# Dilated attention on one core: probabilities turned round by a matmul with a diagonal matrix of the reciprocal sums

## The chip, the cores and the metric

The kernel runs on one core of one Trainium2 chip. The time is device microseconds (us) of one execution, as the median of several runs. The engines named below are TensorE (PE; its weight loads are shown as PEld), VectorE (DVE), ScalarE (ACT), GpSimd (POOL) and SyncE (SP), which only issues transfers here.

## The reference, cut to what matters

The program is one inference step of a two-layer decoder: a layer of dilated attention and a layer of a state-space model, each followed by a SwiGLU. There are 512 prompt tokens, and 8 sample sequences of 8 tokens with caches of up to 2048 keys. The change lies in the attention. Its heart, in the reference:

```python
for g, (win, dil) in enumerate(((128, 1), (512, 4), (2048, 16))):
    s = einsum('bqhd,bqkhd->bqhk', q, k_gathered) * HEAD_DIM ** -0.5
    s = where(valid, s, -inf)
    lse = logsumexp(s, axis=-1)
    o = einsum('bqhk,bqkhd->bqhd', exp(s - lse), v_gathered)
    outs, lses = outs + [o], lses + [lse]
wts = softmax(stack(lses), axis=0)
o = einsum('gbqh,gbqhd->bqhd', wts, stack(outs))
```

Weighting the three groups by their softmax denominators is the same as one softmax over the keys of all three groups together. The kernel computes it so: one row maximum, one exponential and one sum for all keys of a query, and then one product with the values.

## The kernel before

All data are fp32. The program goes through stages in order: normalisation and the q, k, v projections, which also score the sample queries against the cached keys; attention; the output projection with the first feed-forward layer; the state-space layer; the second feed-forward layer. Projections split each fp32 operand into two parts and run three matmuls (`mm6`, L106). The attention stage lies at about 309 to 455 us of the profiled span.

**Prompt attention** (`prompt_pair`, L615) handles one pair of heads. For each of four residues r of the position modulo 4 (128 queries), PE writes a tile of scores S, 128 queries by 512 keys, for each head (L629, L632, L636). DVE adds the mask and takes the row maximum in one instruction (L641). Then `expnorm` (L606) negates and scales the maximum on DVE (L608), takes the exponential with a row sum on ACT (L610), the reciprocal on DVE (L612), and multiplies the 128 by 512 tile by it on DVE (L613). PE turns the four 128 by 128 blocks round (L645) with `te.transpose` against the identity, because the product with the values needs the keys on the partitions. ACT copies the first half of the result out (L646), DVE the second (L648). PE multiplies by the values (L652 for groups 1 and 2 inside the loop over r, L658 for group 0 behind it). There are 4 pairs, 4 residues and 2 heads, so 32 tiles and 128 transposes.

**Sample attention** (`decode`, L662) handles one of 8 sequences. Scores of all cached keys stand in `Sall`, 128 rows by 408. The same `expnorm` runs on them, PE turns three blocks of 128 keys and one of 24 (L671, L674), and PE multiplies with 13 blocks of cached values (L698) and one of new ones (L701). The values come from memory through a ring of six tiles (`kc`, up to 512 KB each), seven loads for a sequence (L388).

**Products.** For sequences 5 to 7 the scores of the widest group are still to be made here: `products` (L392) loads keys and a broadcast query, 512 KB each, into a second ring of four tiles. POOL multiplies them (L397) and DVE sums (L399). Four such parts make one sequence, which `close2` ends with a transpose on PE (L410).

The loop at L725 writes decode, prompt pair (with one product part ahead of each r), decode, four times. The order in which each engine's queue runs is not this order: the program is built with a scheduler that lays out all queues ahead of time by its own estimate of each instruction's duration. Each engine then runs its queue strictly in order, and SP issues transfers strictly in order.

Of the kernel before, what the change touches and what calls it, by code (L numbers as in the profile page):

```python
# [8 lines left out]
F32 = mybir.dt.float32  # L9
# [3 lines left out]
AF = mybir.ActivationFunctionType  # L13
OP = mybir.AluOpType
# [17 lines left out]
SCALE = HD ** -0.5  # L32
# [352 lines left out]
def cache_tile(nc, A, pool_, name, gi, b, c0, n, kv):  # L385
    t = pool_.tile([128, 2, 512], F32, name=name)[:, :n]
    st = STRIDE[gi]
    nc.sync.dma_start(t, dram(A[CACHES[gi]], (b * WIN[gi] + c0) * 1024 + kv * 512, [[st * 1024, 128], [1024, n], [1, 512]]))  # L388
    return t
# [200 lines left out]
def attn_phase(nc, tc, A, es, L):  # L590
    v, s, g, te = nc.vector, nc.scalar, nc.gpsimd, nc.tensor
    ident, pool = L["ident"], L["pool"]
    qT, kT, vt, vscr, att, Sall, mx3, mp, kst = (L[x] for x in ("qT", "kT", "vt", "vscr", "att", "Sall", "mx3", "mp", "kst"))
    ca = es.enter_context(pool("ca"))
    wk = es.enter_context(pool("wka", bufs=2))
# [7 lines left out]
    for t in Pz:  # L603
        g.memset(t, 0.0)

    def expnorm(sm, mx):  # L606
        nm = wk.tile([128, 1], F32, name="nm")
        v.tensor_scalar(nm, mx, -SCALE, None, op0=OP.mult)  # L608
        den = wk.tile([128, 1], F32, name="den")
        s.activation(sm, sm, AF.Exp, bias=nm, scale=SCALE, accum_out=den)  # L610
        rd = wk.tile([128, 1], F32, name="rd")
        v.reciprocal(rd, den)  # L612
        v.tensor_scalar(sm, sm, rd, None, op0=OP.mult)  # L613

    def prompt_pair(hp, fill):  # L615
        O = pO.tile([128, 4, 4, 32], F32, name="O")
        P0 = [wk.tile([128, 2, 4, 4, 32], F32, name=f"P0_{h}", bufs=1) for h in range(2)]
        for r in range(4):
            fill()
            P12 = {}  # L620
            S2 = [pS.tile([128, 512], F32, name="S") for _ in range(2)]
            half = [slice(0, 64), slice(64, 128)]
            for b in range(4):
                for h in range(2):
                    hs = half[h]
                    q = qT[0][hs, hp, r * 128 + b * 32:r * 128 + b * 32 + 32]
                    if b:
                        k = kT[0][hs, hp, (b - 1) * 128:(b + 1) * 128]
                        te.matmul(S2[h][b * 32:b * 32 + 32, 0:256], q, k, start=True, stop=True, tile_position=(h * 64, b * 32))  # L629
                    else:  # L630
                        k = kT[0][hs, hp, 0:128]
                        te.matmul(S2[h][0:32, 0:256].rearrange("p (a c) -> p a c", a=2), q, k[:, None, :].to_broadcast([64, 2, 128]), start=True, stop=True)  # L632
            for gi in (1, 2):
                sl = slice(r * 128, r * 128 + 128)
                for h in range(2):
                    te.matmul(S2[h][:, (gi + 1) * 128:(gi + 2) * 128], qT[gi][half[h], hp, sl], kT[gi][half[h], hp, sl], start=True, stop=True)  # L636
            for h in range(2):
                S = S2[h]
                sm = wk.tile([128, 512], F32, name="sm", bufs=3)
                mx = wk.tile([128, 1], F32, name="mx")  # L640
                v.tensor_tensor_reduce(sm, S, mp[:, r, :], 1.0, -3e38, OP.add, OP.max, mx)  # L641
                expnorm(sm, mx)
                pt = pP.tile([128, 4, 128], F32, name="pt")
                for c in range(4):
                    te.transpose(pt[:, c, :], sm[:, c * 128:(c + 1) * 128], ident)  # L645
                s.activation(P0[h][:, :, :, r, :], pt[:, 0:2, :].rearrange("p a (b i) -> p a b i", b=4), AF.Copy)  # L646
                p12 = wk.tile([128, 2, 128], F32, name="P12", bufs=3)
                v.tensor_copy(p12, pt[:, 2:4, :])  # L648
                P12[h] = p12
            for gi in (1, 2):  # L650
                for h in range(2):
                    te.matmul(O[h * 64:h * 64 + 64, r], vt[gi][:, r, (2 * hp + h) * 64:(2 * hp + h + 1) * 64], P12[h][:, gi - 1, :], start=gi == 1 and r == 0, stop=False, skip_group_check=True)  # L652
        for b in range(4):
            for pv in (1, 0):
                if b == 0 and pv == 0:
                    continue
                for h in range(2):
                    te.matmul(O[h * 64:h * 64 + 64, :, b, :], vt[0][:, b - 1 + pv, (2 * hp + h) * 64:(2 * hp + h + 1) * 64],  # L658
                              P0[h][:, pv, b], start=False, stop=True, skip_group_check=True)
        s.activation(att[:, hp, :T].rearrange("p (b i r) -> p r b i", b=4, r=4), O, AF.Copy)  # L660

    def decode(b):  # L662
        Z = Pz[b % 2]
        P = Sall[:, b].rearrange("p a b -> p (a b)")
        mx = wk.tile([128, 1], F32, name="mx")
        v.tensor_reduce(mx, mx3[:, b, :], AX.X, OP.max)
        expnorm(P, mx)
        P = Sall[:, b]
        pt = pD.tile([128, 4, 128], F32, name="Sd")
        for c in range(3):  # L670
            te.transpose(pt[:, c, :], P[:, c, 0:128], ident)  # L671
        pw = dk.tile([128, 24], F32, name="pw")
        v.tensor_copy(pw.rearrange("p (a b) -> p a b", a=3), P[:, :, 128:136])
        te.transpose(pt[:24, 3, :], pw, ident)  # L674
        pa = dk.tile([128, 4, 32], F32, name="pa")
        s.activation(pa, pt[:, 0, :].rearrange("p (a c) -> p a c", a=4), AF.Copy)
        pn = dk.tile([24, 128], F32, name="pn")
        s.activation(pn, pt[:24, 3, :], AF.Copy)
        for gi, u0, n in ((1, 0, 4), (2, 4, 8)):
            for h in range(2):  # L680
                for m in range(8 // n):
                    j0 = h * 8 + m * n
                    base = Z[:, u0, :, j0:j0 + 1]
                    o = bass.AP(tensor=base.tensor, offset=base.offset, ap=[list(base.ap[0]), [32, 4], [129, n]])
                    v.tensor_copy(o, pt[:, gi, :].rearrange("p (a c) -> p a c", a=4)[:, :, j0:j0 + n])
        vn = dk.tile([24, 512], F32, name="vn", bufs=2)
        for gi in range(3):
            nc.sync.dma_start(vn[gi * 8:gi * 8 + 8, :], vscr[gi, b * 8:b * 8 + 8, :])
        O = pD.tile([128, 128], F32, name="Sd")
        u = 0  # L690
        for gi in (0, 1, 2):
            for c0 in range(0, UNITS[gi], 2):
                w = min(2, UNITS[gi] - c0)
                vc = cache_tile(nc, A, kst, "kc", gi, b, c0, w, 1)
                for c in range(w):
                    for hp in range(4):
                        pz = pa[:, hp, :] if u == 0 else Z[:, u - 1, hp, :]
                        te.matmul(O[hp * 32:hp * 32 + 32, :], pz, vc[:, c, hp * 128:hp * 128 + 128], start=u == 0, stop=False, tile_position=(0, hp * 32), skip_group_check=True)  # L698
                    u += 1
        for hp in range(4):  # L700
            te.matmul(O[hp * 32:hp * 32 + 32, :], pn[:, hp * 32:hp * 32 + 32], vn[:, hp * 128:hp * 128 + 128], start=False, stop=True, tile_position=(0, hp * 32), skip_group_check=True)  # L701
        os_ = dk.tile([128, 128], F32, name="os")
        s.activation(os_, O, AF.Copy)
        ot = pD.tile([128, 4, 32], F32, name="Sd")
        te.transpose(ot.rearrange("p a b -> p (a b)"), os_, ident)
        q0 = T + b * 8
        for h in range(2):
            hs = slice(h * 64, h * 64 + 64)
            v.tensor_copy(att[hs, :, q0:q0 + 8], ot[hs, :, h * 8:h * 8 + 8])
# [15 lines left out]
    for hp in range(4):  # L725
        decode(2 * hp)
        prompt_pair(hp, score2)
        decode(2 * hp + 1)
# [623 lines left out]
```

## Time and profile before

| what | value |
|---|---|
| median of 3 runs | 1567.87 us (1565.44 to 1578.34) |
| the profiled execution, its own time | 1561.29 us |
| its span from first to last instruction | 1559.5 us |
| attention stage within the span | about 309 to 455 us |
| mean granted TensorE clock | 0.990 |

In the views, a group row has the line, engine, operation, output and inputs, sizes, count, and after the bar the busy time in us, the mean of one in ns, and the idle time ahead of it with what ended it. A row of waits says which engine and line waited for what: us in total, times, longest. Matmul ends are modelled and a matmul's duration includes the time it takes through the array, so consecutive ones overlap; what the next one has to wait is seen in the distance from start to start.

### The profile page before, as it was taken

The numbers are of one execution on the slowest core, as the hardware profiler recorded it, in microseconds if no ns is written. First come the engines' busy times: TensorE is split into PE (matmuls) and PEld (weight loads), VectorE is DVE, ScalarE is ACT, GpSimd is POOL, SyncE is SP. The second block draws the span as 40 slices with busy tenths as digits, with TensorE's granted clock in tenths as the row PEclk, the third lists the DMA queues.
The fourth block names the chain that finished last, engine by engine and source line by source line (L and its number), as shares of the span: only waits on it lengthen the run. The fifth ranks groups of instructions, "written<-read, shape, count | busy, mean of one in ns | idle before, by whom it ended". The sixth has DMA issues, their size and how long they took to land. (4 is left out here: it accounts for less than half of the span.)

```text
span 1559.5 us, 28913 instructions
## 1 busy us (share of the span) xinstructions
PE 1504.5 (96%) x12010; PEld 1393.8 (89%) x12010; DVE 917.9 (59%) x1661; ACT 522.4 (33%) x774; POOL 318.3 (20%) x343
## 2 busy tenths in 40 slices
PE   8989899889979999999999999999999999999998
PEld 6878688656669999999999999999999999999998
DVE  5898864558726865388878667764443333333332
ACT  4524344634415221122222254443342212221222
POOL 2000102333203014745335420021111001000100
PEclk9999999999989999999999999999999999999999
DMA  7497753798785556589667765964655555442212
GB/s 248 143 375 234 264 187 109 239 357 285 275 274 195 189 189 223 202 283 315 213 241 243 237 227 181 287 204 170 215 189 189 188 188 220 153 145 82 82 62 81
DMA packets 194323, 326.79 MB, mean 210 GB/s; under 512 B 39568, under 2 KB 137104, under 8 KB 192656
## 3 DMA queue, kind: packets, MB, share of 16 engines
q1 hardware_dynamic: 184112, 305.86, 57.8%
q10 hardware_dynamic: 10080, 19.08, 3.5%
q8 instruction: 94, 1.54, 0.4%
q14 instruction: 37, 0.30, 0.1%
HBM read 291.31 MB, written 120.88 MB: 264 GB/s over the span
## 5 line engine op out<-in xcount | busy, mean ns | idle before, releaser
L100 DVE TENSOR_TENSOR wlo<-raw,whi 128x1024 fp32r<-128x1024 f32 x200 | 246.4, 1233 | 269.1 <-ACT whi L99 263.3
L106 PE MATMUL acc<-xgl,whi 128*128 128x288 f32 x1760 | 378.6, 296 | 1.0 <-DVE xgl L171 1.0
L106 PE MATMUL acc<-xgh,wlo 128*128 128x288 f32 x1760 | 377.7, 296 | 0.0
L106 PE MATMUL acc<-xgh,whi 128*128 128x288 f32 x1760 | 377.0, 296 | 0.1
L99 ACT ACTIVATE whi<-raw 128x1024 fp32r<-128x1024 f32 x200 | 208.1, 1042 | 503.3 <-PE acc L106 405.0
L106 PEld LDWEIGHTS acc<-xgl,whi 128*128 128x128 f32 x1760 | 282.6, 188 | 2.5 <-DVE xgl L171 1.3
L106 PEld LDWEIGHTS acc<-xgh,wlo 128*128 128x128 f32 x1760 | 282.7, 188 | 0.6 <-issue 0.2
L106 PEld LDWEIGHTS acc<-xgh,whi 128*128 128x128 f32 x1760 | 281.7, 188 | 0.5 <-DVE gt L789 0.3
L791 POOL TENSOR_TENSOR gt<-gt,rstd 128x576 f32<-128x576 f32 x44 | 77.1, 1754 | 431.8 <-ACT gt L790 431.7
L106 PE MATMUL acc<-hh,whi 128*128 128x288 f32 x704 | 151.3, 296 | 0.0
L106 PE MATMUL acc<-hh,wlo 128*128 128x288 f32 x704 | 151.2, 295 | 0.0
L106 PE MATMUL acc<-hl,whi 128*128 128x288 f32 x704 | 150.9, 295 | 0.0
L352 PE MATMUL acc<-wlo,xh 128*128 128x512 f32 x288 | 115.6, 403 | 3.2 <-DVE wlo L100 3.2
L351 PE MATMUL acc<-whi,xh 128*128 128x512 f32 x288 | 108.8, 402 | 5.0 <-ACT a L567 3.9
L106 PEld LDWEIGHTS acc<-hh,wlo 128*128 128x128 f32 x704 | 113.2, 188 | 0.2 <-issue 0.2
L106 PEld LDWEIGHTS acc<-hl,whi 128*128 128x128 f32 x704 | 113.0, 188 | 0.2 <-issue 0.2
L353 PE MATMUL acc<-whi,xl 128*128 128x512 f32 x288 | 113.1, 398 | 0.0
L106 PEld LDWEIGHTS acc<-hh,whi 128*128 128x128 f32 x704 | 113.1, 188 | 0.0
L191 POOL TENSOR_TENSOR ssum<-ssum,sq 128x576 f32<-128x576 f32 x21 | 36.1, 1720 | 181.0 <-ACT sq L190 181.0
L351 PEld LDWEIGHTS acc<-whi,xh 128*128 128x128 f32 x288 | 54.9, 192 | 18.3 <-ACT a L567 4.7
L352 PEld LDWEIGHTS acc<-wlo,xh 128*128 128x128 f32 x288 | 55.3, 192 | 15.4 <-DVE wlo L100 4.2
L803 DVE TENSOR_TENSOR xT<-acc,xT 128x576 f32<-128x576 f32 x48 | 36.2, 754 | 49.2 <-PE acc L106 49.2
(349 smaller groups left out, 2010.8 us busy)
## 6 DMA issues: line engine op xcount, KB each, us to landing
o_kv_s<-cache_kv_w SPq DMA_DIRECT2D x64, 1020.0 KB
kc<-cache_kv_w SPq DMA_DIRECT2D x96, 512.0 KB
raw<-ffn_w_gate SPq DMA_DIRECT2D x44, 512.0 KB
raw<-ffn_w_up SPq DMA_DIRECT2D x44, 512.0 KB
raw<-ffn_w_down SPq DMA_DIRECT2D x40, 512.0 KB
raw<-w_qkv SPq DMA_DIRECT2D x36, 512.0 KB
kc<-qscr SPq DMA_DIRECT2D x32, 512.0 KB
o_kv_s<-cache_kv_w SPq DMA_DIRECT2D x16, 1008.0 KB
```

The source lines that it names most:

```text
L99: s.activation(hi, raw, AF.Copy)
L100: mark[0] = v.tensor_tensor(lo, raw, hi.bitcast(F32), OP.subtract)
L106: te.matmul(ps[:, c, :HN], w, x[:, c * HN:(c + 1) * HN], start=first and i == 0, stop=last and i == 2)
L191: g.tensor_tensor(self.ss, self.ss, sq, OP.add)
L351: te.matmul(ps[t], ah, wh[:, k2, :], start=k == 0, stop=False)
L352: te.matmul(ps[t], ah, wl[:, k2, :], start=False, stop=False)
L353: te.matmul(ps[t], al, wh[:, k2, :], start=False, stop=k == KT - 1)
L791: g.tensor_tensor(t, t, nin.r, OP.mult)
L803: v.tensor_tensor(xv, ps[m][:, :, :HN], xv, OP.add)
```

## The change

In `expnorm` the scaling of the whole tile by the reciprocal sum is gone. In its place DVE scales the 128 by 128 identity by the reciprocal sums, which gives a diagonal matrix `dg`, and PE's four `te.transpose` calls become ordinary `te.matmul` calls with `dg` as the moving operand. Turning round and normalising are one step. In the prompt part, the masking instruction now also multiplies by minus the scale and takes the minimum, so that it gives the negated maximum directly; the exponential then uses a scale of -1. In the sample part the negation stays as its own instruction. No transfer is added or removed.

```diff
-    def expnorm(sm, mx):
-        nm = wk.tile([128, 1], F32, name="nm")
-        v.tensor_scalar(nm, mx, -SCALE, None, op0=OP.mult)
+    def expnorm(sm, nm, scale):
         den = wk.tile([128, 1], F32, name="den")
-        s.activation(sm, sm, AF.Exp, bias=nm, scale=SCALE, accum_out=den)
+        s.activation(sm, sm, AF.Exp, bias=nm, scale=scale, accum_out=den)
         rd = wk.tile([128, 1], F32, name="rd")
         v.reciprocal(rd, den)
-        v.tensor_scalar(sm, sm, rd, None, op0=OP.mult)
+        dg = wk.tile([128, 128], F32, name="dg", bufs=3)
+        v.tensor_scalar(dg, ident, rd, None, op0=OP.mult)
+        return dg
...
-                mx = wk.tile([128, 1], F32, name="mx")
-                v.tensor_tensor_reduce(sm, S, mp[:, r, :], 1.0, -3e38, OP.add, OP.max, mx)
-                expnorm(sm, mx)
+                nm = wk.tile([128, 1], F32, name="nm")
+                v.tensor_tensor_reduce(sm, S, mp[:, r, :], -SCALE, 3e38, OP.add, OP.min, nm)
+                dg = expnorm(sm, nm, -1.0)
                 pt = pP.tile([128, 4, 128], F32, name="pt")
                 for c in range(4):
-                    te.transpose(pt[:, c, :], sm[:, c * 128:(c + 1) * 128], ident)
+                    te.matmul(pt[:, c, :], sm[:, c * 128:(c + 1) * 128], dg, start=True, stop=True)
...
-        expnorm(P, mx)
+        nm = wk.tile([128, 1], F32, name="nm")
+        v.tensor_scalar(nm, mx, -SCALE, None, op0=OP.mult)
+        dg = expnorm(P, nm, SCALE)
...
-            te.transpose(pt[:, c, :], P[:, c, 0:128], ident)
+            te.matmul(pt[:, c, :], P[:, c, 0:128], dg, start=True, stop=True)
...
-        te.transpose(pt[:24, 3, :], pw, ident)
+        te.matmul(pt[:24, 3, :], pw, dg, start=True, stop=True)
```

The scheduler lays the queues of the attention stage out anew; ahead of the last cache scores and from the first matmuls of the output projection on, PE's queue is unchanged. Two places in the queues matter below. (In the new kernel the exponential of `expnorm` is L608, the reciprocal L610 and the diagonal L612, and from L667 on a line of the kernel before stands two lines further down.)

The first is DVE's queue in the first head pair. The kernel before has one product part (the two sums of L399) between the work on the second and third residue:

```order
391 L608 TENSOR_SCALAR nm<-mx 128x1
392 L641 ISA sm,mx<-S,mp 128x512
393 L641 ISA mx 128x1
394 L709 COPY att<-Sd 64x4x8 x2
395 L608 TENSOR_SCALAR nm<-mx 128x1
396 L612 RECIPROCAL rd<-den 128x1
397 L399 TENSOR_REDUCE P_3317<-kc 128x4x2 x2
398 L613 TENSOR_SCALAR sm<-sm,rd 128x512
```

The new kernel has all four parts of sequence 5 there, ahead of the masking of the second residue's second head and of the first two copies of L648:

```order
383 L641 ISA sm,nm<-S,mp 128x512
384 L641 ISA nm 128x1
385 L610 RECIPROCAL rd<-den 128x1
386 L399 TENSOR_REDUCE P_3318<-kc 128x4x2 x2
387 L612 TENSOR_SCALAR dg<-ident,rd 128x128
388 L399 TENSOR_REDUCE P_3318<-kc 128x4x2 x6
389 L641 ISA sm,nm<-S,mp 128x512
390 L641 ISA nm 128x1
391 L648 COPY P_3356<-pt 128x256
392 L648 COPY P_3373<-pt 128x256
```

What moved: three more product parts stand ahead of the rest of the second residue.

The second is the end of PE's queue in the attention stage. The kernel before has two whole sample sequences behind the last prompt products (L658):

```order
1395 L658 MATMUL O<-P_1_4783,vt_3165 64x4x32
1396 L698 MATMUL Sd<-kc,pa 32x128 x4
1397 L698 MATMUL Sd<-kc,Pz_3203 32x128 x48
1398 L701 MATMUL Sd<-vn,pn 32x128 x4
1399 L705 MATMUL Sd<-ident,os 128x128
1400 L671 MATMUL Sd<-ident,Sall 128x128 x3
1401 L674 MATMUL Sd<-ident,pw 24x128
1402 L698 MATMUL Sd<-kc,pa 32x128 x4
1403 L698 MATMUL Sd<-kc,Pz_3204 32x128 x48
1404 L701 MATMUL Sd<-vn,pn 32x128 x4
1405 L705 MATMUL Sd<-ident,os 128x128
1406 L106 MATMUL acc_5178<-ath,whi 128x288 x2
```

The new kernel has one:

```order
1399 L658 MATMUL O<-P_1_4766,vt_3165 64x4x32
1400 L700 MATMUL Sd<-kc,pa 32x128 x4
1401 L700 MATMUL Sd<-kc,Pz_3204 32x128 x48
1402 L703 MATMUL Sd<-vn,pn 32x128 x4
1403 L707 MATMUL Sd<-ident,os 128x128
1404 L106 MATMUL acc_5154<-ath,whi 128x288 x2
```

What moved: the seventh sequence's products with the values stand further up, between prompt work.

## The prediction

> **What bounds the kernel now.** I read the page first, to see which engine is full, then the attention stage in windows, then who waits there. On the page PE is busy 96% of the span, DVE 59%. The change touches only the attention stage, so the stage decides. Its windows (busy us and count of each engine, granted clock, DMA share, GB/s):
>
> ```profile
> core 0: us, PE busy (x) PEld busy (x) DVE busy (x) ACT busy (x) POOL busy (x), PEclk, DMA share, GB/s
> 309.00:327.00 18.00, 11.10 (x198) 8.33 (x198) 3.62 (x25) 5.47 (x11) 3.44 (x17) 0.81 1.03 377
> 327.00:437.00 110.00, 104.41 (x1445) 68.73 (x1449) 84.55 (x305) 48.68 (x132) 30.00 (x20) 0.98 0.83 293
> 437.00:455.00 18.00, 10.93 (x206) 6.78 (x206) 1.15 (x9) 0.98 (x4) 0.00 (x0) 0.81 0.85 283
> ```
>
> There are three parts. Up to 327 us PE has gaps and the transfers run at 377 GB/s; from 327 to 437 PE is busy 104 of 110 us; behind that it has gaps again. DVE is at 85 of 110 us in the middle, high but second. Since a matmul's shown duration holds its way through the array, I checked the middle in the timeline (start, duration):
>
> ```profile
> 356.10 0.66 PE L645 MATMUL pt<-ident,sm 128*128 128x128 f32 x4
> 356.69 0.40 PE L632 MATMUL S<-kT,att 64*32 64x256 f32 x1
> ...
> 357.25 0.71 PE L636 MATMUL S<-kT,qT 64*128 64x128 f32 x4
> 357.89 0.33 PE L410 MATMUL Sd<-ident,P 128*128 128x128 f32 x1
> ```
>
> Each piece starts before the one ahead of it is out of the array. What PE waits for, in the middle window (first eight rows) and in the last one (two rows):
>
> ```profile
> PE S L632 <- DVE mx L641: 1.3, 2, 1.0
> PE pt L645 <- ACT pa L676: 1.2, 1, 1.2
> PE O L652 <- DVE P L648: 0.8, 1, 0.8
> PE O L652 <- DVE nm L608: 0.6, 1, 0.6
> PE pt L645 <- DVE sm L613: 0.6, 1, 0.6
> PE pt L645 <- ACT P L646: 0.6, 1, 0.6
> PE Sd L698 <- DMA kc<-cache_kv_w: 0.2, 1, 0.2
> PE pt L645 <- DVE pw L673: 0.2, 1, 0.2
> ...
> PE Sd L698 <- DMA kc<-cache_kv_w: 5.7, 6, 2.4
> PE Sd L705 <- ACT os L703: 0.9, 2, 0.5
> ```
>
> In 110 us PE waits 3.5 us for DVE, 1.8 for ACT and 0.2 for a transfer: 5.5 us. Nearly all of the rest is PE's own work. So I read the middle as bound by PE, and the end, 5.7 us, by the loads of cached values.
>
> **The change on PE.** The question is what an ordinary fp32 matmul costs beside a transpose. Rows of the whole span and of the stage:
>
> ```profile
> L645 PE MATMUL pt<-ident,sm 128*128 128x128 f32 x128 | 20.3, 289 | 2.6 <-ACT pa L676 1.2 <-DVE sm L613 0.6 <-ACT P L646 0.6
> L652 PE MATMUL O<-P,vt 128*64 128x128 f32 x128 | 16.7, 291 | 1.5 <-DVE P L648 0.8 <-DVE nm L608 0.6
> ...
> 666.27 0.60 PE L1039 MATMUL aux<-ident,wr 128*128 128x128 f32 x4
> ...
> L1039 PE MATMUL aux<-ident,wr x64: 270/272/329, 666.3 to 866.6; 128*128 128x128 f32 x64
> ...
> 988.95 0.34 PE L1174 MATMUL aux<-U,Tc 128*128 128x72 f32 x2
> ...
> 995.83 0.39 PE L1175 MATMUL acc<-Xt,Vc 128*128 128x72 f32 x2
> ```
>
> L645 stands in the code 4 x 4 x 2 x 4 = 128 times and has 128 records: a transpose is one instruction. L652 stands there 4 x 4 x 2 x 2 = 64 times and has 128 records: an ordinary fp32 matmul is two. The price of a transpose comes from L1039: four take 0.60 us, the last of them 0.272, so the step is (0.60 - 0.272) / 3 = 0.109 us. The price of an ordinary one with a full 128 by 128 stationary operand comes from the stretch of L1174 and L1175: from the first to the last row there are 32 calls, of L1174 and L1175 in turn, so 31 steps: (995.83 - 988.95) / 31 = 0.222 us. These have 72 moving columns instead of 128; two instructions of a transpose's step, which has 128, would be 0.218, so I see no reason for a very different price. So a new call takes 0.113 us more. [...] There are 128 calls in the prompt part and 8 x 4 = 32 in the sample part, so PE gets 160 x 0.113 = +18.1 us. The bounds are 0, if the second instruction runs in gaps that PE has anyway, and 18.1, if none does. Eight calls, those of the first and last sequence, stand beside waits for transfers: -0.9.
>
> **The change on DVE and ACT.**
>
> ```profile
> L613 DVE TENSOR_SCALAR sm<-sm,rd 128x512 f32<-128x512 f32 x32 | 22.4, 701 | 0.5
> L399 DVE TENSOR_REDUCE P<-kc 128x8 f32<-128x512 f32 x24 | 15.2, 677 | 2.0 <-POOL kc L397 2.0
> L608 DVE TENSOR_SCALAR nm<-mx 128x1 f32<-128x1 f32 x40 | 5.5, 143 | 0.1
> L613 DVE TENSOR_SCALAR Sall<-Sall,rd 128x408 f32<-128x408 f32 x8 | 4.4, 556 | 0.1
> ```
>
> Removed: 22.4 + 4.4 us of L613, and 32 of the 40 negations, 32 x 0.143 = 4.6 us; together 31.4. Added: 40 diagonals of 128 by 128. No row shows one. The nearest rows are L608 at 0.143 and L613 at 0.556; the two forms of L613 differ by 0.145 us for 104 elements, so 128 elements come to 0.556 - 280 x 0.0014 = 0.17. I take 0.2 (bounds 0.14 and 0.56): 8 us. DVE is relieved of about 23 us. The exponential with another scale and the minimum in place of the maximum keep their sizes, so I cost them at nothing; ACT, at 49 of 110 us, would hide a small change.
>
> But DVE's relief is worth only what PE waits for it. The chain from scores to transposes gets shorter by 0.143 + 0.5 us for each tile, and of the 5.5 us in the middle I let 3.0 go (bounds 0 and 5.3). What is late next is PE itself.
>
> **The order.** At the end, one sample sequence instead of two stands behind the prompt work, so the loads of the seventh can run under it. Of the 5.7 us of load waits and 0.9 of the last copies I let 4.0 go (bounds 0 and 6.6). At the front, the new kernel starts prompt scores ahead of the first sequence's values, and puts four product parts into DVE's queue ahead of the second residue. Queued behind them on DVE are a masking and the two copies (L648) for which PE's value products wait. What the parts take:
>
> ```profile
> L397 POOL TENSOR_TENSOR kc<-kc 128x1024 f32<-128x1024 f32 x12 | 28.4, 2371 | 48.4 <-DMA kc<-qscr 36.8 <-ACT P L646 11.5
> L698 PE MATMUL Sd<-kc,Pz 128*32 128x128 f32 x768 | 29.8, 294 | 6.0 <-DMA kc<-cache_kv_w 5.9
> ```
>
> Four parts load eight tiles of 512 KB, 4.2 MB; at 293 GB/s that is 14.3 us, and a multiplication (2.4) and two sums (1.4) follow the last: 18 us. PE has the first sequence's values to run there, 29.8 / 8 = 3.7 us, and eight blocks of turning, 8 x 0.222 = 1.8. If nothing else covers it, the hold is 18 - 5.5 = 12.5 us. On the other side, an earlier start of the scores can give back at most what PE waits at the front for loads of keys:
>
> ```profile
> PE pt L484 <- DMA kc<-cache_kv_w: 6.2, 2, 3.4
> ```
>
> The bounds are -6.2 and +12.5. The product parts that come early are not in the way later, and the loads are the same in sum, so I take 0.
>
> The sum: 18.1 - 0.9 - 3.0 - 4.0 + 0 = +10.2 us. On the profiled execution, whose own time is 1561.29 us for a span of 1559.5, that is 1571.5. The median of the three runs is 1567.87, 6.6 us above it; I add to the median: 1578.
>
> **The rivals.**
>
> *DVE sets the pace, and the kernel gets faster.* For it speaks that DVE is at 85 of 110 us and that ACT waits for DVE's negation often:
>
> ```profile
> ACT sm L610 <- DVE nm L608: 31.0, 22, 5.5
> ```
>
> If the second instruction of a new call slips into gaps on PE (those between its pieces, which the wait rows leave out), the 18.1 us vanish and what PE waits for is won: up to 5.5 in the middle and 6.6 at the end, 12.1 us, 1556. It decides where a call costs less than 12.1 / 160 = 0.076 us more than a transpose. Against it stand the rows at 0.113 and PE's short waits. Chance 0.10, taken over -5 to -12.
>
> *Hidden.* PE's addition falls into waits for loads, since the first 20 us of the stage move 377 GB/s and the middle 293; the transfers, not PE, then set the end. Against it: one wait of 0.2 us for a transfer in the middle. -5 to +4, about 1567. Chance 0.13.
>
> *Fourfold.* [...] Chance 0.02.
>
> *The front holds.* The product parts keep DVE and then PE for the 12.5 us worked out: 10.2 + 12.5 = +22.7, 1590. For it speaks the strict order of the queues; against it, that PE gets ahead elsewhere. Taken over +15 to +23. Chance 0.17.
>
> The forecast, PE pays for most of the second instructions, +4 to +15, has 0.58.
>
> **How the numbers follow.** A change of under 1% (15.7 us) can't be told from none with three runs that lie 13 us apart. Faster by more than that needs more than all of PE's waits: 0.03, out of the first rival. Slower by more than that is nearly all of the last rival, the fourfold one and a little of the forecast's upper edge: 0.21. Within 1%: 0.76. The range reaches from the lower side of "hidden" (-5, 1563) to the upper of "the front holds" (+23, 1591); outside lie most of the first rival and the fourfold one, 0.12, and a little for the unknown terms.
>
> **What would show it.** The rows of the turning should have 256, 48 and 16 records in place of 128, 24 and 8, with about 0.22 us from call to call. DVE's busy time in the stage should fall by about 23 us and the waits of PE for it by some 3. The load waits ahead of the output projection should shrink to 1 or 2 us. The first matmul of the output projection should come about 10 us later; all behind it should be unmoved. A wait of many us of PE for L648 or L641 in the first head pair would be the front's hold. A start-to-start step near 0.11 us per call would prove the price wrong.

## The result, and the profile after

The changed kernel takes 1593.12 us (median of four, 1592.34 to 1599.11) where the kernel before, run beside it, takes 1572.14 us: 21.0 us more, a ratio of 1.0155 with a 95% interval of 1.0117 to 1.0193. In a later session, with more executions (e13 below), the medians are 1595.34 and 1573.55 us and the ratio 1.0131 (1.0093 to 1.0169). The ratios leave out a run that lies more than 1.5% above the fastest one of its kernel. The forecast was +10.2 us; the loss is about twice that, and close to the +22.7 of the rival "the front holds".

The profiled execution after took 1599.11 us for a span of 1597.0, 37.8 us more than the profiled one before. That is more than the medians differ by, and the sections below show most of why: the two executions spent different times at half clock.

First the page's windows of the kernel after. The columns are those of the windows in the prediction: busy us and count of each engine, granted clock, DMA share, GB/s. The stage was cut where its character changes:

```profile
321.00:345.00 24.00, 18.08 (x173) 11.42 (x174) 6.71 (x29) 4.44 (x11) 6.14 (x12) 0.52 0.83 282
345.00:353.00 8.00, 1.92 (x52) 1.57 (x48) 1.81 (x3) 0.00 (x0) 2.23 (x2) 0.71 0.86 284
353.00:366.00 13.00, 13.00 (x80) 8.55 (x74) 6.92 (x18) 2.67 (x7) 6.13 (x7) 0.50 1.04 386
366.00:386.00 20.00, 20.00 (x222) 14.33 (x222) 17.33 (x53) 8.68 (x24) 7.09 (x3) 0.99 0.59 202
386.00:490.00 104.00, 99.45 (x1420) 72.14 (x1417) 47.98 (x192) 36.73 (x99) 10.21 (x8) 1.00 0.66 230
```

And the same stage of the kernel before:

```profile
317.00:325.00 8.00, 6.11 (x88) 4.86 (x91) 0.62 (x4) 1.79 (x3) 0.61 (x3) 0.57 1.05 386
325.00:333.00 8.00, 7.89 (x154) 4.21 (x147) 3.96 (x15) 2.28 (x7) 0.00 (x0) 1.00 1.05 393
333.00:356.00 23.00, 21.11 (x212) 13.57 (x210) 21.62 (x71) 11.29 (x31) 9.38 (x4) 1.00 0.67 245
356.00:456.00 100.00, 88.23 (x1336) 58.81 (x1334) 60.66 (x232) 36.67 (x102) 20.61 (x16) 0.95 0.85 294
```

The first head pair ends at 356 us before and at 386 after, 30 us later. Of these, 6 us lie ahead of its first scores, which start at 325.7 us before and at 332.0 after; in e13, the changed kernel once more, they start at 326.9, so these 6 us belong to this execution and not to the change. From its first score to its last product the pair takes 31 us before, 54 after and 51 in e13. The rest of the stage, which holds three quarters of the new second instructions, takes 100 us before and 106 after (the output projection starts at 456 and at 492 us). So most of the loss is at the front. The granted clock there is 0.50 to 0.52 for most of 45 us, where the front before has a low clock only in the 8 us from 317.

What PE waits for from 309 to 385 us in the kernel after:

```profile
PE Sd L700 <- DMA kc<-cache_kv_w: 6.1, 1, 6.1
PE pt L484 <- DMA kc<-cache_kv_w: 5.0, 1, 5.0
PE Sd L673 <- DVE dg L612: 1.3, 1, 1.3
PE Sd L488 <- DVE mx L493: 1.1, 2, 0.5
PE S L632 <- DVE mx L493: 0.4, 1, 0.4
```

Both long waits are for transfers: one for a late tile of cached keys, and one for the seventh value tile of the first sequence. Only the second is new: for key tiles the kernel before waits 6.2 us, in two waits (the prediction shows the row). No wait for L648 or L641 of the first head pair is among them. The value ring holds six tiles. In the new order PE makes the scores of two residues before it touches the first value tile, so the seventh can only be asked for late. In e13 PE waits 9.3 us for that tile, with a clock of 0.88 from 350 us to the pair's end at 378, and the pair takes 51 us all the same: half clock alone is not the front's loss.

Finally the turning itself (the tile's view, then three rows of PE's timeline: start, duration), and the diagonals:

```profile
L645 PE MATMUL pt<-dg,sm x256: 274/275/583, 341.8 to 481.0; 128*128 128x128 f32 x128
...
354.40 3.35 PE L645 MATMUL pt<-dg,sm 128*128 128x128 f32 x14
...
369.32 1.16 PE L645 MATMUL pt<-dg,sm 128*128 128x128 f32 x8
370.40 0.62 PE L629 MATMUL S<-kT,att 64*32 64x256 f32 x2
```

```profile
L612 DVE TENSOR_SCALAR dg<-ident,rd 128x128 f32<-128x128 f32 x40 | 19.4, 485 | 13.0 <-PE pt L645 12.0
```

There are 256 records for 128 calls: two instructions each, as forecast. At full clock four calls take 370.40 - 369.32 = 1.08 us up to the next piece. In the kernel before, four transposes took 356.69 - 356.10 = 0.59. So a call costs 0.49 / 4 = 0.122 us more, and 160 calls 19.6 us; the prediction had 0.113 and 18.1. At half clock seven calls (354.40 to 357.68) take 0.47 us each.

### The profile page after: what moved, and what is told of

Read it like the earlier page. It is cut to its first block, busy times and chain, and to the rows that moved or that the text cites. A ratio compares the mean times of both kernels' runs of the same rounds, so it can differ in the third digit from the quotient of the medians.

```text
span 1597.0 us, 29201 instructions
## 1 busy us (share of the span) xinstructions
PE 1540.0 (96%) x12170; PEld 1424.1 (89%) x12170; DVE 910.7 (57%) x1629; ACT 522.6 (33%) x774; POOL 316.8 (20%) x343
## 5 line engine op out<-in xcount | busy, mean ns | idle before, releaser
L353 PEld LDWEIGHTS acc<-whi,xl 128*128 128x128 f32 x288 | 55.5, 193 | 11.2
```

Of the source, the lines that this page charges most:

```text
L353: te.matmul(ps[t], al, wh[:, k2, :], start=False, stop=k == KT - 1)
```

## The experiments

Two theories were set against each other at first. "Price": the loss is the second instruction of 160 matmuls. "Front": the loss is the order at the front of the stage, and that order comes from where the tiles lie in memory. The second has a reason in the build. The three `dg` tiles take 1536 bytes per partition, and everything allocated behind them moves up by that much. The accumulator of the product parts, P2, lay on an operand of the projections before; now it lies in part on tiles that the scoring of cached keys still uses, as Q2 does. A buffer that comes free later gives the scheduler another order; which of the overlaps decides was not tried. As built, with one `dg` buffer (512 bytes) the order of the front is like that of the kernel before, with two (1024 bytes) like that of the kernel after; neither was timed.

**e1, the tiles shifted and nothing else.** The kernel before, with unused room at the end of two tiles:

```diff
-        P0 = [wk.tile([128, 2, 4, 4, 32], F32, name=f"P0_{h}", bufs=1) for h in range(2)]
+        P0 = [wk.tile([128, 1216], F32, name=f"P0_{h}", bufs=1)[:, :1024].rearrange("p (a b r i) -> p a b r i", a=2, b=4, r=4) for h in range(2)]
```

> The kernel before with no operation changed: the two tiles P0 of the prompt attention are each 768 bytes per partition longer than they need be, 1536 bytes together, as much as the three diagonal tiles of the changed kernel take. That shifts the sample part's small tiles and the ring of the product parts to the addresses that they have in the changed kernel, and the order that the scheduler then writes has four product parts ahead of the second residue's second masking, as there. Theory 'front' (the changed kernel's loss comes from the order at the front of the attention stage, and the order comes from where the tiles lie): +12 to +30 us, about as much as the whole change (+21), and the end of the first head pair about 25 to 30 us later than before. Theory 'price' (the loss is the second instruction of 160 matmuls): within 3 us of the kernel before.

Measured: 1589.22 against 1566.54 us, ratio 1.0121 (1.0078 to 1.0165), about +19 us by the ratio and +23 by the medians. On another chip (e15) it was 1.0109 (1.0066 to 1.0151). No operation differs from the kernel before, so the new order is worth nearly the whole change by itself, and "price" as the only cause falls. Windows of e1, and PE's longest waits from 320 to 393 us:

```profile
320.00:343.00 23.00, 18.51 (x201) 12.24 (x205) 7.66 (x32) 4.44 (x11) 6.67 (x12) 0.55 0.85 286
343.00:351.00 8.00, 1.79 (x44) 0.99 (x32) 1.65 (x4) 0.00 (x0) 2.35 (x1) 0.67 0.91 303
351.00:393.00 42.00, 42.00 (x216) 23.95 (x210) 25.84 (x85) 12.34 (x33) 17.22 (x11) 0.50 0.72 246
393.00:483.00 90.00, 84.41 (x1335) 58.04 (x1331) 50.41 (x211) 36.28 (x98) 5.57 (x6) 0.99 0.74 249
```

```profile
PE Sd L698 <- DMA kc<-cache_kv_w: 6.2, 1, 6.2
PE pt L484 <- DMA kc<-cache_kv_w: 3.6, 1, 3.6
```

PE waits 6.2 us for the seventh value tile. Then it is busy 42.00 of 42 us, with no listed wait of its own, at a granted clock of 0.50. The first head pair takes those 42 us; in the kernel before its turnings and products took the 23 us from 333. The shift brings the new order of the end too, with one sample sequence behind the prompt work, and there time comes back: the rest of the stage takes 90 us, with 100 in the kernel before (at a clock of 0.99 and 0.95). So the front by itself costs more than the +19.

**e2, the changed kernel with its diagonals allocated last.**

```diff
+    dgp = es.enter_context(pool("dgp", bufs=3))
...
-        dg = wk.tile([128, 128], F32, name="dg", bufs=3)
+        dg = dgp.tile([128, 128], F32, name="dg")
```

> The changed kernel with its three diagonal tiles in a pool of their own, allocated behind the product parts' ring: every other tile lies where it lay before, and the order of the front is nearly that of the kernel before. All operations are those of the changed kernel. Theory 'front': the loss of the front goes; what is left is the second instructions less what DVE's relief gives, -5 to +11 us against the kernel before. Theory 'price': +18 to +21 us, as the changed kernel.

Measured: 1577.50 us, ratio 1.0076 (1.0047 to 1.0106), about +12 us. All other tiles lie where they lay, the front is back, and what is left is close to the +10.2 that the prediction gave with the order term at zero. That is partly luck: by the table below some 4 us of less time at half clock are in it, and the rest is +15. Its windows and PE's waits from 327 to 471 us:

```profile
321.00:333.00 12.00, 9.80 (x202) 6.29 (x197) 3.64 (x18) 3.31 (x7) 1.27 (x7) 1.00 1.02 357
333.00:361.00 28.00, 28.00 (x292) 19.55 (x286) 22.08 (x65) 12.16 (x33) 9.40 (x4) 1.00 0.76 268
361.00:471.00 110.00, 103.27 (x1463) 73.37 (x1460) 55.46 (x209) 37.79 (x101) 20.50 (x16) 0.98 0.79 263
...
PE Sd L701 <- DMA kc<-cache_kv_w: 4.2, 5, 1.5
...
PE pt L646 <- DVE dg L613: 0.3, 1, 0.3
```

From 321 us on the front runs at full clock, and PE waits 0.3 us for a diagonal.

**e3, the second instruction alone.** `te.transpose(…, ident)` became `te.matmul(…, ident, start=True, stop=True)` at the three places, and DVE's scaling and negations stayed.

> The kernel before with one edit: the 160 turnings of the probabilities are ordinary fp32 matmuls with the identity in place of transposes; the scaling on DVE and the negations stay. The front's order is close to the kernel before. If PE pays for each second instruction (0.113 us by the prediction): +15 to +18 us. If the second instructions run in gaps that PE has anyway: -2 to +5 us. Theory 'front' leaves room for anything up to +10.

Measured: 1576.57 us, ratio 1.0050 (1.0019 to 1.0081): +8 us by the ratio, +10 by the medians. That is less than the 15 to 18 expected. The table below has one reason; another is that the end has the new order here too (from the last prompt product to the output projection PE takes 8.4 us in e3, 20.7 in the kernel before), so this run does not hold the second instruction quite alone.

**e4, the negated maximum alone.** The masking instruction of the kernel before got `-SCALE`, `3e38` and `OP.min`, and 32 negations went.

> The kernel before with the other part alone: the masking instruction of the prompt part gives the negated maximum itself, and 32 negations go (32 x 0.143 = 4.6 us of DVE). Turnings and scaling as before. Both theories: the chain from scores to turning is shorter by 0.14 us in each of 32 tiles, and PE waits 3.5 us for DVE in the whole middle, so -3 to 0 us; a change beyond 3 us either way would be the order again, which differs from the second residue on.

Measured: 1570.67 us, ratio 1.0013 (0.9983 to 1.0044): nothing that can be told from zero. The relief of DVE that this part brings has no price here.

**e5, the product parts taken apart.** The changed kernel, with each part's sums behind the previous residue's copy:

```diff
-            fill()
+            if hp == 0 and r:
+                with tc.issue_after(last.ins):
+                    fill()
+            else:
+                fill()
...
-                v.tensor_copy(p12, pt[:, 2:4, :])
+                last = v.tensor_copy(p12, pt[:, 2:4, :])
```

> The changed kernel with one rule more on the order: in the first head pair the sums of a product part come on DVE behind the copy (L648) of the residue before, so that each residue has one part ahead of its masking and not four. All operations stay. Theory 'hold' (what the prediction's rival said: four parts keep DVE, and PE waits for its maskings and copies): 10 to 15 us of the changed kernel's loss go, which leaves +8 to +12 us against the kernel before. Theory 'clock' (PE first waits for two transfers, a key tile and the seventh value tile, and then runs at half clock with no long wait): those two waits stay, so the loss stays, +17 to +25 us.

Measured: 1590.22 us, ratio 1.0129 (1.0070 to 1.0187), the same as the changed kernel (1.0131). DVE's waits for POOL's product, kernel after from 335 to 386 us (first row) and e5 from 309 to 386 (second), and PE's two waits in e5 (last two):

```profile
DVE P L399 <- POOL kc L397: 16.0, 4, 6.8
```

```profile
DVE P L399 <- POOL kc L397: 3.3, 1, 3.3
...
PE pt L484 <- DMA kc<-cache_kv_w: 6.1, 1, 6.1
PE Sd L704 <- DMA kc<-cache_kv_w: 5.6, 1, 5.6
```

The hold on DVE went, from 16.0 us to 3.3, and no time came back that the runs can show; the interval reaches down to +11 us, so a few us could hide in it. In the changed kernel itself no long wait of PE for DVE stands in the first pair. So the mechanism that the rival "the front holds" named, product parts that keep DVE, is not what costs the time, or hardly. The two transfers stayed, and so did the half clock.

**e6 and e7, work put into the wait.** To e1 was added, between the sixth and the seventh value tile, 20 ordinary matmuls (e6) or 32 transposes (e7) of the identity:

```diff
+                if b == 0 and u == 11:
+                    D = pO.tile([128, 512], F32, name="O")
+                    for _ in range(20):
+                        with tc.issue_after(last.ins):
+                            last = te.matmul(D[:, 0:128], ident, ident, start=True, stop=True)
```

> The kernel of e1 (tiles shifted, transposes as before) with work added: 20 ordinary fp32 matmuls of the identity with itself (128 by 128 by 128, into the accumulator that the first head pair uses later) between the sixth and the seventh value tile of the first sequence, where PE waits 6.5 us for the seventh. At half clock they take 20 x 0.43 = 8.5 us, at full clock 4.5. Theory 'clock': PE stays busy through the wait, the clock rises and holds, and the first head pair takes some 25 us instead of 42: 12 to 20 us of e1's loss go, 0 to +8 us against the kernel before. Theory 'hold', or a clock that does not depend on this: the added work costs 0 to 4 us, +19 to +27 us.

> As e6, but the added work is 32 transposes of the identity in place of 20 ordinary matmuls: 32 x 0.213 = 6.8 us at half clock, 3.5 at full. It tells what kind of work lifts the clock. If any work on PE does: as e6, 0 to +8 us against the kernel before, and the same granted clock behind it. [...]

Measured: ratios 1.0112 (1.0049 to 1.0175) and 1.0092 (1.0061 to 1.0123). Neither is what "clock" expected, but the added work did not fill the wait. In e6:

```profile
330.00:342.00 12.00, 12.00 (x159) 9.84 (x160) 5.22 (x23) 2.65 (x8) 4.28 (x2) 0.86 0.69 193
342.00:350.00 8.00, 1.43 (x22) 1.02 (x20) 1.86 (x3) 0.00 (x0) 2.37 (x2) 0.83 0.92 301
350.00:385.00 35.00, 33.66 (x185) 19.94 (x178) 25.25 (x69) 9.84 (x27) 15.28 (x11) 0.50 0.76 267
...
PE Sd L704 <- DMA kc<-cache_kv_w: 6.6, 1, 6.6
```

PE did the added matmuls before 343 us and then waited 6.6 us as it had, and the clock fell during that wait (0.83 in the 8 us from 342, 0.50 in the 35 behind them). In e7 the 32 transposes ran at full clock (3.7 us from 342), a wait of 3.9 us was left, and the clock was at 0.50 behind it until about 365 us and not until 390.

**e8, the same 20 matmuls in the changed kernel.**

> The changed kernel with the same 20 ordinary matmuls between the sixth and the seventh value tile of the first sequence, where it waits 6.1 us. Theory 'clock': the stretch from 349 to 366 us goes at full clock, which is 17 us of half clock, so some 6 to 9 us go: +12 to +18 us against the kernel before. Theory 'hold', or a clock that does not depend on this: no gain, +21 to +28 us.

Measured: 1601.97 us, ratio 1.0191 (1.0118 to 1.0263): no gain, a miss for "clock". Here the work did fill more than half of the wait: PE waits 2.7 us for the seventh tile where the changed kernel waits 6.1. Yet the clock falls all the same (profiled execution, 1615.37 us, the longest of the four):

```profile
353.00:394.00 41.00, 40.17 (x193) 26.16 (x196) 21.32 (x67) 9.99 (x29) 16.23 (x11) 0.51 0.62 215
```

**e9, the second residue's scores put into the wait.** Starting from e1, the first sequence's chain is issued behind the first residue's, and its products up to the sixth tile ahead of the second residue's scores, with the seventh behind them:

```diff
+            if hp == 0 and r == 1:
+                d0 = decode_g(0)
+                gx.enter_context(tc.issue_after(next(d0).ins))
...
+                if u == 11:
+                    yield last
```

> The kernel of e1 with another order on PE at the front: the second residue's scores (24 matmuls of the first head pair) stand between the sixth and the seventh value tile of the first sequence, and that sequence's own chain is issued behind the first residue's, so that PE has work of its own where it waited 6.5 us for the seventh tile. No work is added. Theory 'clock' (a long wait drops PE to half clock, and the spell then lasts through the first head pair): the wait of 6.5 us goes, and most of the spell from 345 to 393 us with it; of e1's loss of about 20 us, 10 to 18 go, 0 to +10 us against the kernel before. If the clock wanders whatever the waits are: +15 to +22 us.

Measured: 1585.54 against 1573.61 us, ratio 1.0069 (1.0046 to 1.0093), about +11 us where e1 had +17 to +19. PE's longest waits from 315 to 400 us and two windows of e9:

```profile
PE pt L484 <- DMA kc<-cache_kv_w: 7.0, 1, 7.0
PE pt L661 <- DVE sm L613: 3.1, 1, 3.1
PE Sd L717 <- DMA kc<-cache_kv_w: 1.3, 1, 1.3
...
349.00:367.00 18.00, 18.00 (x104) 10.61 (x105) 12.10 (x40) 5.97 (x17) 7.87 (x7) 0.53 0.79 281
367.00:376.00 9.00, 9.00 (x95) 6.14 (x94) 8.84 (x28) 4.23 (x13) 2.36 (x1) 1.00 0.52 171
```

The wait for the seventh tile went from 6.2 to 1.3 us, and the spell at half clock behind it from 42 us to 18. A part of the loss came back, a little less than "clock" expected; the key tile's wait stayed, and a turning now waits for DVE.

**e10, the same edit in the changed kernel.**

> The changed kernel with the same edit as e9. Theory 'clock': the front's loss goes for the most part, and it comes near to e2 (the changed kernel with its tiles where they were before), +8 to +15 us against the kernel before. If the clock wanders whatever the waits are: +20 to +25 us.

Measured: 1606.20 us, ratio 1.0208 (1.0168 to 1.0247): worse than the changed kernel, a miss for both theories. Its longest waits, from 315 to 400 us, show what came in place of the seventh tile's:

```profile
PE pt L484 <- DMA kc<-cache_kv_w: 7.2, 1, 7.2
PE S L642 <- DVE nm L657: 2.6, 1, 2.6
PE pt L661 <- DVE mx L682: 2.3, 1, 2.3
PE Sd L719 <- DMA kc<-cache_kv_w: 2.3, 1, 2.3
```

From 349 to 373 us its clock is 0.52. So with a shorter wait for the seventh tile the time fell in e9 and did not in e8 and e10: that this wait is what brings the half clock is not shown.

**e11 and e12, an order meant to beat both kernels.** In the kernel before, in each head pair but the first, two groups of turnings come behind a sequence's value products:

```diff
+                gt = gates.get({(0, 0): 2 * hp - 1, (3, 0): 2 * hp}.get((r, h))) if hp else None
+                with tc.issue_after(gt.ins) if gt is not None else ExitStack():
```

> The kernel before with a rule on the order that is meant to beat both: in each head pair but the first, the turnings of the first residue come behind the value products of the odd sequence before, and those of the fourth residue behind those of the even one. So one sequence instead of two stands behind the prompt work, as in the changed kernel, and the ring of value tiles is freed earlier. In e2 and e3 PE spends 12.2 and 8.4 us from the last product of the prompt to the output projection where the kernel before spends 20.7. If that tail is worth its 8 to 12 us: -4 to -10 us. If the waits only move to the middle: -3 to +5 us.

> As e11, but the odd sequence's products are wanted one residue later (ahead of the turnings of the second residue instead of the first), which gives their tiles some 6 us more to land. If e11 waits for value tiles in the middle, this waits less: -4 to -12 us; else the same as e11 within 3 us.

Measured: e11 1571.11 against 1573.61 us, ratio 0.9982 (0.9952 to 1.0011); e12 1583.46 us, ratio 1.0048 (1.0015 to 1.0082), a miss for both of its expectations. Neither beats the kernel before.

**e13 to e15, one chip, and the time at half clock.** By then it was open why e1 (+19) and e2 (+12) together should only make +21.

> The changed kernel once more, unchanged, on one chip with the next two and with the kernel before, so that their times and their time at half clock can be set side by side. [...]

> e1 and e3 together: the kernel before with its two P0 tiles lengthened by 768 bytes each, and with the 160 turnings as ordinary fp32 matmuls with the identity; DVE's scaling and negations stay. If the two losses simply add up: +19 and +8 make +27 us, with some 90 us at half clock as in e1. If ordinary matmuls shorten the spells that transposes let last (e3 had 35 us at half clock and the kernel before 47): 45 to 65 us at half clock and +18 to +24 us, as the changed kernel.

> e1 once more on this chip, for its time at half clock beside that of e14: +17 to +24 us against the kernel before and 80 to 100 us at half clock, as in its first runs.

Measured: 1.0131 (1.0093 to 1.0169), 1.0156 (1.0089 to 1.0223) and 1.0109 (1.0066 to 1.0151). Each execution's mean granted clock gives its time at half clock, as (1 - clock) x 2 x span; in these traces the granted clock is either 1.00 or 0.50 at any moment. Over 182 executions in 20 groups (each kernel, and the kernel before apart by chip), measured from each group's mean, a microsecond more at half clock goes with 0.36 us more time; the correlation is 0.87. If the factor also holds from one kernel to another, which was not tried, the medians split as follows (us against the kernel before on the same chip):

| kernel | time | at half clock | of it clock | rest |
|---|---|---|---|---|
| before, on the three chips of the rows below | 0 | 46.9, 59.7, 56.5 | 0 | 0 |
| e1, shift | +22.7 | 92.1 | +16.3 | +6.4 |
| e15, shift again | +18.0 | 92.3 | +12.9 | +5.1 |
| e9, shift, wait filled | +11.9 | 83.9 | +8.7 | +3.2 |
| e4, negated maximum | +4.1 | 54.8 | +2.8 | +1.3 |
| e3, second instruction | +10.0 | 34.6 | -4.4 | +14.4 |
| e2, diagonals last | +11.0 | 34.7 | -4.4 | +15.4 |
| e13, changed kernel | +21.8 | 54.2 | -0.8 | +22.6 |
| e14, shift and second instruction | +25.6 | 67.1 | +3.8 | +21.8 |

(e1 to e4 belong to the first chip, e9 to the second, e13 to e15 to the third; for e14 the medians of the three runs that its ratio uses. e13 came within its forecast of +20 to +25 us, e15 as expected, e14 between its two readings.) The rests add up: 5 to 6 for the shift, 15 for the change without the shift, 22 to 23 for both. The time at half clock does not: the shift has 36 to 45 us more than the kernel before and e2 and e3 have 12 less, which would make 24 to 33 more for both together; e14 has 11 more and the changed kernel 2 less. So by this split the changed kernel loses hardly anything to half clock beyond what the kernel before loses, and e1 most of what it loses. With four to ten runs in a row the intervals of the ratios reach 4 to 10 us to either side, so the split tells sizes only roughly.

## Why the prediction was wrong, point by point

**The step that failed is the order term, taken as 0 with bounds of -6.2 and +12.5.** The front costs: the shift that brings its order costs 17 to 19 us alone (e1, e15), and 9 to 11 us on top of the change's own 11 to 12 (e2 against the changed kernel). In the profiles the first pair takes 21 to 24 us more (51 and 54 us for 31), of which its 32 new prompt calls explain 4. The prediction saw the place, two ends of the price and a rival for it, but took 0 with the argument that what comes early is not in the way later. As a cost it weighed only what stands in DVE's queue. That PE makes prompt scores ahead of the first sequence's values it did say, but only as something that could give time back. What it did not weigh is a ring of six tiles for seven loads: with the scores of two residues ahead of the first value tile, the seventh comes late. A row for that stands in the trace of before, among PE's waits from 317 to 336 us, where the first sequence's value products run in the kernel before:

```profile
PE Sd L698 <- DMA kc<-cache_kv_w: 0.2, 1, 0.2
```

That wait is short: those products start at 322.3 us, ahead of the first prompt scores, and run on between them until 332 while tiles still come in.

**The rival "the front holds" had the sum right (+22.7) by luck, and the mechanism wrong.** It had PE wait for DVE behind four product parts. PE waited for transfers: 5.0 us for a key tile, as it also did before, and 6.1 us for the seventh value tile, which is new. With the parts apart (e5) the loss stayed.

**The time at half clock was no term at all.** Durations were taken at full clock, although the windows of before showed 0.81 ahead of 327 us and behind 437. The profiled execution of before, with a mean clock of 0.990, had (1 - 0.990) x 2 x 1559.5 = 31 us at half clock, where the executions beside e1 to e4 had 47; the profiled one after had 64. So by the factor above 33 x 0.36 = 12 us of the 37.8 between the two profiles are the clock. Between the medians of the two kernels it is nearly nothing (-0.8 in the table).

**The price was right, as PE's own time.** Two instructions per call, 0.122 us more each for a forecast of 0.113; 19.6 us for 18.1. No run shows it as time of the kernel by itself, since e3 changes the end's order too. The factor between an ordinary call and a transpose is (1.08 / 4) / (0.59 / 4) = 1.8 as they stand in the program. No run shows a factor of four: the fourfold rival is out.

**The -3.0 for PE's waits for DVE was about right in size, and wrong in its cause.** The 3.5 us of waits went to 0.5 in e2, and to 1.7 behind the first pair of the changed kernel. But they went in e3 too, where DVE keeps all its work; PE's waits there from 327 to 475 us:

```profile
PE Sd L698 <- DMA kc<-cache_kv_w: 4.9, 4, 2.0
PE acc L106 <- ACT ath L740: 1.3, 1, 1.3
PE pt L645 <- DVE sm L613: 0.6, 1, 0.6
PE Sd L705 <- ACT os L703: 0.5, 1, 0.5
```

The likely reason is that PE, with more work of its own, comes later for what DVE makes; no run shows it apart. The relief of DVE shows no gain: e4, with 4.6 us of it, is not faster than the kernel before, and e2, with all of it, is not faster than e3, with none (1577.50 and 1576.57 us). It was also smaller than forecast: a diagonal took 0.485 us on average for an estimate of 0.2 (within its bounds), so the net relief is 31.4 - 19.4 = 12 us and not 23. The average hides two kinds: 32 of the 40 diagonals took 0.27 to 0.29 us, and seven of the eight that met a multiplication on POOL (L397) took 0.42 to 2.42, the longest ones ending 0.1 us behind it.

**The -4.0 at the end was right, as a wait.** Load waits behind the last prompt products, kernel after (480 to 493 us):

```profile
PE Sd L700 <- DMA kc<-cache_kv_w: 1.9, 1, 1.9
```

That is 1.9 us, where before had 5.7. What it is worth in time no run shows by itself: e11 makes the same move in the kernel before and comes out at 0.9982 (0.9952 to 1.0011).

## What to carry to other kernels

An edit that adds a small tile can change the whole order of a scheduled program, because tiles behind it come to lie on others; before its arithmetic is judged, put the new tile where it moves nothing, or shift the old kernel's tiles by as much and time that. When an order changes, ask each engine in turn what it now does first, and whether a ring of buffers still refills in time. Compare mean granted clocks before reading a difference of 1% out of two profiles.

## What the runs showed of the hardware that was not expected

**A wait of PE, at times a short one, can be followed by tens of microseconds at half clock, although PE is busy throughout.** In e1 it was 42 us at 0.50 behind a wait of 6.2; in e15 the same again:

```profile
350.00:392.00 42.00, 42.00 (x215) 24.22 (x214) 25.07 (x84) 12.06 (x32) 17.21 (x11) 0.50 0.73 247
```

In e11, whose front is that of the kernel before, a single wait of 1.4 us for a masking stood ahead of such a spell (windows and PE's longest wait from 327 to 371 us):

```profile
327.00:340.00 13.00, 11.56 (x171) 6.53 (x171) 9.09 (x29) 4.22 (x12) 4.85 (x2) 1.00 1.04 381
340.00:371.00 31.00, 30.83 (x177) 19.14 (x175) 16.41 (x58) 9.76 (x25) 6.13 (x3) 0.51 0.47 160
...
PE S L634 <- DVE mx L643: 1.5, 2, 1.4
```

The same mix of work ran at full clock in the kernel before, in the 23 us from 333. The kernel before has a wait of 1.0 us for the same instruction (at 348 us) with no such spell: its clock is 1.00 from 333 to 356 us. So a short wait is not always followed by one. The half clock is real and not only a reading: a call of the turning took 0.47 us in it and 0.27 outside.

**Whether the kind of matmul matters for how long a spell lasts is open.** The medians at half clock are 34.7 and 34.6 us with ordinary matmuls (e2, e3) and 46.9 with transposes on the same chip, and 67.1 (e14, ordinary) and 92.3 (e15, transposes) with the shift. By these medians there is less half clock with ordinary matmuls. Single spells do not show that: in e8, with ordinary matmuls, one lasts the 41 us shown above, and in e7, with transposes, PE is back at full clock after some 16 us.
